# One plain gate/up step in place of two at the head of the second feed-forward half

## The chip, the cores and the metric

The kernel runs on one core of a Trainium2 chip. The metric is the device time of one launch in microseconds (us). The kernel before took 1154.8 us, the median of three runs from 1154.61 to 1155.35 us; the execution that was profiled took 1154.97 us.

Four engines do the work. PE multiplies matrices and writes to PSUM banks of 128 x 512 numbers; PEld is its weight loading. DVE does elementwise work on two operands, ACT does activations and casts, POOL little here. SP only issues transfers between device memory and on-chip memory. Each engine runs its own instructions strictly in the order in which the program lists them, and waits on semaphores for the others.

## The reference

One decoder layer with 512 tokens of width 1024, in float32:

```
x = x + 0.5 * swiglu(rms_norm(x, ffn1_norm), w_gate1, w_up1, w_down1)
h = rms_norm(x); z = h @ w_in            # gates, gMLP, q, k, v
m = sigmoid(g_a) * (y_a @ P_A) + sigmoid(g_b) * (y_b @ P_B)
x = x + m @ w_out
x = x + 0.5 * swiglu(rms_norm(x, ffn2_norm), w_gate2, w_up2, w_down2)

swiglu(h) = (silu(h @ w_gate) * (h @ w_up)) @ w_down     # hidden width 2816
```

The change is in the last line, the second feed-forward half.

## The kernel before

**Arithmetic.** A float32 product is made of three PE passes: each operand is split into a high part (`hi`, a cast on ACT, line 139) and a rest (`lo = src - hi`, a subtraction on DVE, line 140), and hi x hi, hi x lo and lo x hi are accumulated (`mm3`, lines 124 to 127; in `quad`, line 324).

**A feed-forward half** is `ffn`. The hidden width 2816 is 22 blocks of 128, taken two at a time: 11 steps, numbered q = 0 to 10. A step computes gate and up for two blocks and leaves the activated product in `a_hi[q]`, `a_lo[q]`. After the steps 0 to 3, 4 to 7 and 8 to 10 the eight down projections (line 375) follow. Loads of weights are issued by SP into `w_raw` tiles.

There are two kinds of step, and the argument `plain` says how many of the first steps are of the first kind:

- `plain_quad(q)`: for each of the two blocks, gate and up are accumulated over all 8 slices of the input with `mm3`, 512 columns a matmul: 2 x 8 x 2 x 3 = 96 matmuls of 512 columns. It needs the scaled input `xg_hi`, `xg_lo`, four loads and four splits of weights.
- `quad(q)`: a Strassen-Winograd scheme with 2 x 2 blocks (two halves of the input width, two halves of the tokens; gate and up play the other pair). It makes seven products in place of eight, each of 24 matmuls of 256 columns: 168 in all. Four of the products are with `S0` to `S3`, sums of quarters of the scaled input; four of the seven weights are sums (`total`, line 311, `w_sum` tiles, on DVE). Seven weights are split. The products come in the order A11, S1, S2, A22, S0, A12, S3. The first product goes into bank `a`, is copied out (`kept`, line 331, on ACT), and S2 is then accumulated on top of it in the same bank; S1 goes into bank `c`.

The sums S0 to S3 are made once for a half, by `add_sums` (lines 214 to 230): for each of four slices kt, one ACT scaling (line 222), four DVE operations of 256 columns (lines 224 to 227) into a tile `sums`, and then a split of 1024 columns into `s_hi` (ACT) and `s_lo` (DVE). The calls stand behind the last plain step (lines 372 to 374); one split holds all four sums of its slice, so the product S1 needs `s_hi` and `s_lo` of all four slices.

**What stands around the change.** The mixing stage ends with eight output projections (`add_out`), which leave the new input in tiles `x1` and its scaled parts in `xg_hi`, `xg_lo`. `plain_quad(0)` starts at once. Before its second block it runs `norm_scale` (lines 198 to 204), which makes `r_bc`, the reciprocal norm of each token: two PE matmuls, two ACT operations and three on DVE (lines 159 to 161). At its end each plain step does per block a DVE multiplication by `r_bc` (line 299), a Silu on ACT (line 300), a DVE multiplication (line 301), and then the split into `a_hi`, `a_lo`.

**What sets the order.** The code is written in program order, and a scheduler of the framework distributes it: by priorities and modelled durations it fixes at build time the order on each engine. So an operation of a later step can be placed ahead of one of an earlier step, and matmuls of two products can alternate. On the chip that order is then fixed. Weight tiles (`w_hi`, `w_lo`) are taken in turn from four places, `w_raw` from six, `w_sum` from two.

Of the kernel before, what the change touches and what calls it, by code (L numbers as in the profile page):

```python
# [58 lines left out]
def decoder_block(  # L59
# [434 lines left out]
    x1 = []  # L494
# [462 lines left out]
    with tc.tile_pool(name="ff2", bufs=1) as ff2:  # L957
        def finish2(j, y, ts):
            nc.sync.dma_start(out=out[:, j, ts], in_=y)

        def again2(t, j):
            nc.sync.dma_start(out=t, in_=x2_dram[j])

        ffn(ff2, gu2, dn2, 2, x1, finish2, None, {0: (norm_scale, lambda: None)}, again2, 2)


# [79 lines left out]
```

## Time and profile before

| | us |
|---|---|
| median of three runs | 1154.8 |
| profiled execution | 1154.97 |
| its span, first to last instruction | 1153.3 |
| PE busy | 1145.2 (99%) |
| DVE busy | 845.9 (73%) |
| ACT busy | 590.7 (51%) |
| POOL busy | 28.6 (2%) |
| outside the span | 1.7 |

The busy time of PE is modelled from pipelined matmuls that overlap each other: the time that a matmul costs is the distance from its start to the start of the next. The same holds in small for DVE and ACT, where a row begins a little before the one ahead of it ends. The granted clock is full (1.00) in all stretches up to the end of the kernel's work. In the second half, `plain_quad(0)` starts at 802.34 us, `plain_quad(1)` at 825.09 us, `quad(2)` at 847.38 us and `quad(3)` at 867.29 us.

### The profile page before, as it was taken

Reading aid. Unit: us, or ns where it says so; the run is one execution under the profiler, and the core shown is the slowest. Engines: PE = TensorE matmul, PEld = TensorE weight load, DVE = VectorE, ACT = ScalarE, POOL = GpSimd, SP = SyncE. Lnnn points to the kernel's source line nnn. Section 1 sums busy time; section 2 is a strip of 40 time slices with the busy share of each in tenths; the row PEclk is TensorE's granted clock in tenths of the full one; section 3 lists DMA queues with packets and bytes.
Section 4 is the critical chain, followed back from the end, with each engine's and each line's share of the span. In section 5 each row is a group of like instructions: output and inputs, shape, how many; then the busy total and the mean of one; then the engine's idle time right before and its main releaser. Section 6 shows DMA issues by size and latency. Waiting matters only on the chain.

```text
span 1153.3 us, 16684 instructions
## 1 busy us (share of the span) xinstructions
PE 1145.2 (99%) x6568; PEld 996.8 (86%) x6568; DVE 845.9 (73%) x1374; ACT 590.7 (51%) x856; POOL 28.6 (2%) x57
## 2 busy tenths in 40 slices
PE   8999999999999999999999999999999999999998
PEld 7898899989987888888878887888899899988997
DVE  6985489768876767867878976655887369877874
ACT  6653356414544554667587966334545235523440
POOL 0000000000002000000000000000000000000000
PEclk9999999999999999999999999999999999999999
DMA  8144132623324323222212124334424223541222
GB/s 276 53 132 143 55 116 75 227 64 110 90 94 147 118 74 92 74 92 74 74 55 73 56 79 160 92 123 163 152 74 147 73 74 110 166 148 67 87 82 73
DMA packets 46861, 122.08 MB, mean 106 GB/s; under 512 B 4560, under 2 KB 5856, under 8 KB 46784
## 3 DMA queue, kind: packets, MB, share of 16 engines
q1 hardware_dynamic: 44208, 113.26, 30.7%
q0 software_dynamic: 2432, 7.75, 2.0%
q8 instruction: 51, 0.84, 0.3%
q14 instruction: 26, 0.21, 0.1%
q10 hardware_dynamic: 144, 0.01, 0.0%
HBM read 114.72 MB, written 6.29 MB: 105 GB/s over the span
## 4 chain that ended last, share of the span: by engine, by line
PE 95%; ACT 2%; DMA 1%; DVE 1%; issue 0%; SPq 0%; ACTq 0%; DVEq 0%
PE bank_acc L324 20%; PE bank_att L324 11%; PE bank_acc L127 11%; PE bank_acc L125 11%; PE bank_acc L126 11%; PE bank_att L127 5%; PE bank_att L126 5%; PE bank_att L125 5%; PE bank_acc L537 4%; PE bank_acc L539 4%; PE bank_acc L538 4%; DMA w_raw<-in_gu 1%; PE bank_att L667 1%; PE bank_att L668 1%; PE bank_att L695 1%
## 5 line engine op out<-in xcount | busy, mean ns | idle before, releaser
L139 ACT CAST w_hi<-w_raw 128x1024 fp32r<-128x1024 f32 (+2 forms) x192 | 191.8, 1004 | 281.2 <-PE bank_acc L126 91.8
L140 DVE TENSOR_TENSOR w_lo<-w_raw,w_hi 128x1024 fp32r<-128x1024 f32 (+2 forms) x192 | 224.0, 1170 | 78.2 <-ACT w_hi L139 73.3
L139 ACT CAST w_hi<-w_sum 128x1024 fp32r<-128x1024 f32 x72 | 75.5, 1050 | 138.7 <-PE bank_acc L324 62.0
L324 PE MATMUL bank_acc<-s_lo,w_hi 128*128 128x256 f32 x432 | 121.6, 281 | 0.0
L324 PE MATMUL bank_acc<-s_hi,w_hi 128*128 128x256 f32 x432 | 121.5, 281 | 0.0
L324 PE MATMUL bank_acc<-s_hi,w_lo 128*128 128x256 f32 x432 | 121.4, 281 | 0.0
L140 DVE TENSOR_TENSOR w_lo<-w_sum,w_hi 128x1024 fp32r<-128x1024 f32 x72 | 87.6, 1220 | 26.0 <-ACT w_hi L139 26.0
L125 PE MATMUL bank_acc<-xg_hi,w_hi 128*128 128x512 f32 x224 | 89.3, 399 | 1.3 <-ACT w_hi L139 1.3
L127 PE MATMUL bank_acc<-xg_hi,w_lo 128*128 128x512 f32 x224 | 89.2, 398 | 1.0 <-DVE w_lo L140 1.0
L537 PE MATMUL bank_acc<-w_hi,xg_hi 128*128 128x512 f32 x224 | 88.9, 397 | 0.0
L126 PE MATMUL bank_acc<-xg_lo,w_hi 128*128 128x512 f32 x224 | 88.8, 396 | 0.0
L538 PE MATMUL bank_acc<-w_lo,xg_hi 128*128 128x512 f32 x224 | 88.6, 395 | 0.0
L539 PE MATMUL bank_acc<-w_hi,xg_lo 128*128 128x512 f32 x224 | 88.5, 395 | 0.0
L324 PEld LDWEIGHTS bank_acc<-s_hi,w_hi 128*128 128x128 f32 x432 | 81.6, 189 | 0.0
L324 PEld LDWEIGHTS bank_acc<-s_hi,w_lo 128*128 128x128 f32 x432 | 81.7, 189 | 0.0
L324 PEld LDWEIGHTS bank_acc<-s_lo,w_hi 128*128 128x128 f32 x432 | 81.6, 189 | 0.0
L125 PE MATMUL bank_acc<-a_hi,w_hi 128*128 128x512 f32 (+1 forms) x182 | 71.1, 391 | 0.0
L126 PE MATMUL bank_acc<-a_lo,w_hi 128*128 128x512 f32 (+1 forms) x182 | 71.1, 391 | 0.0
L127 PE MATMUL bank_acc<-a_hi,w_lo 128*128 128x512 f32 (+1 forms) x182 | 71.1, 391 | 0.0
L126 PE MATMUL bank_att<-a_lo,w_hi 128*128 128x512 f32 (+1 forms) x176 | 68.7, 391 | 0.0
L125 PE MATMUL bank_att<-a_hi,w_hi 128*128 128x512 f32 (+1 forms) x176 | 68.7, 391 | 0.0
L127 PE MATMUL bank_att<-a_hi,w_lo 128*128 128x512 f32 (+1 forms) x176 | 68.7, 390 | 0.0
(270 smaller groups left out, 2847.2 us busy)
## 6 DMA issues: line engine op xcount, KB each, us to landing
w_raw<-in_gu SPq DMA_DIRECT2D x86, 512.0 KB, 3.8
w_raw<-in_dn SPq DMA_DIRECT2D x32, 512.0 KB, 3.8
w_raw<-in_w_qk SPq DMA_DIRECT2D x16, 512.0 KB, 3.6
w_raw<-in_dn SPq DMA_DIRECT2D x16, 384.0 KB, 3.1
w_raw<-in_w_v SPq DMA_DIRECT2D x8, 512.0 KB, 3.6
w_raw<-in_w_ga SPq DMA_DIRECT2D x8, 512.0 KB, 3.5
w_raw<-in_w_gb SPq DMA_DIRECT2D x8, 512.0 KB, 3.7
w_raw<-in_w_pb SPq DMA_DIRECT2D x8, 512.0 KB, 3.5
```

The costliest lines, as they stand in the source:

```text
L125: nc.tensor.matmul(ps, lhsT=lhi, rhs=rhi, start=first, stop=False)
L126: nc.tensor.matmul(ps, lhsT=lhi, rhs=rlo, start=False, stop=False)
L127: nc.tensor.matmul(ps, lhsT=llo, rhs=rhi, start=False, stop=last)
L139: latest["hi"] = nc.scalar.copy(hi, src)
L140: latest["lo"] = nc.vector.tensor_tensor(lo, src, hi, op=ALU.subtract)
L324: nc.tensor.matmul(o, lhsT=l[:, s], rhs=r, start=first and f == kt == i == 0, stop=kt == HK - 1 and i == 2, skip_group_check=True,)
L537: nc.tensor.matmul(banks[t], lhsT=xg_hi[k][:, ts], rhs=hi[:, s], start=k == 0, stop=False)
L538: nc.tensor.matmul(banks[t], lhsT=xg_hi[k][:, ts], rhs=lo[:, s], start=False, stop=False)
L539: nc.tensor.matmul(banks[t], lhsT=xg_lo[k][:, ts], rhs=hi[:, s], start=False, stop=k == KD - 1)
L667: nc.tensor.matmul(s[m], lhsT=qd[m][:, qs], rhs=kd[m][:, :w], start=True, stop=False)
L668: nc.tensor.matmul(s[m], lhsT=ql[m][:, qs], rhs=kd[m][:, :w], start=False, stop=True)
L695: nc.tensor.transpose(ps[:, j * P : (j + 1) * P], a[:, j * P : (j + 1) * P], ident)
```

## The change

In the second feed-forward half the number of plain steps goes from two to one. Step 0 stays plain; step 1, which was plain, is made by `quad`, and `add_sums` is called behind step 0. Steps 2 to 10, the down projections and the first half, which keeps its two plain steps, are written as before.

```diff
@@ -961,7 +961,7 @@
         def again2(t, j):
             nc.sync.dma_start(out=t, in_=x2_dram[j])
 
-        ffn(ff2, gu2, dn2, 2, x1, finish2, None, {0: (norm_scale, lambda: None)}, again2, 2)
+        ffn(ff2, gu2, dn2, 2, x1, finish2, None, {0: (norm_scale, lambda: None)}, again2, 1)
```

The change moves instructions on all engines from step 1 on. Three places follow.

On PE, the first matmuls with the sums. In the kernel before they are those of product S1 in `quad(2)`, behind the 24 of A11; `w_hi_8033` is the weight of S1:

```order
L324 MATMUL bank_att_7999<-s_hi0_7952,w_hi_8033 128x256 [waits Activation_49]
L324 MATMUL bank_att_7999<-s_lo0_7953,w_hi_8033 128x256
L324 MATMUL bank_att_7999<-s_hi0_7952,w_lo_8034 128x256 [waits DVE_49]
L324 MATMUL bank_att_7999<-s_hi1_7963,w_hi_8033 128x256
L324 MATMUL bank_att_7999<-s_lo1_7964,w_hi_8033 128x256
L324 MATMUL bank_att_7999<-s_hi1_7963,w_lo_8034 128x256
```

In the changed kernel they are in `quad(1)`, again behind the 24 of A11. Slices 0 and 1 of S1, two matmuls of S2 and the one with `s_hi` of slice 2 come first; then, with `w_hi_7898` the weight of S1 and `w_hi_7930`, `w_lo_7931` that of S2:

```order
L324 MATMUL bank_att_7864<-s_lo2_7840,w_hi_7898 128x256 [waits DVE_49]
L324 MATMUL bank_att_7864<-s_hi2_7839,w_lo_7899 128x256
L324 MATMUL bank_acc_7863<-s_hi0_7817,w_lo_7931 128x256 [waits DVE_49]
L324 MATMUL bank_acc_7863<-s_hi1_7828,w_hi_7930 128x256
L324 MATMUL bank_acc_7863<-s_lo1_7829,w_hi_7930 128x256
L324 MATMUL bank_acc_7863<-s_hi1_7828,w_lo_7931 128x256
L324 MATMUL bank_acc_7863<-s_hi2_7839,w_hi_7930 128x256
L324 MATMUL bank_acc_7863<-s_lo2_7840,w_hi_7930 128x256
L324 MATMUL bank_acc_7863<-s_hi2_7839,w_lo_7931 128x256
L324 MATMUL bank_att_7864<-s_hi3_7850,w_hi_7898 128x256 [waits Activation_49]
L324 MATMUL bank_acc_7863<-s_hi3_7850,w_hi_7930 128x256
L324 MATMUL bank_att_7864<-s_lo3_7851,w_hi_7898 128x256 [waits DVE_49]
```

Matmuls of S1 and S2 alternate now, and each slice of the sums has waits of its own. Ahead of the matmul with `s_lo3_7851` stand 44 of the step's 168.

On DVE, what stands between the sums of slice 1 and the last of slice 3, before:

```order
L226 SCALAR_TENSOR_TENSOR sums_7967<-x1_6_7060,neg_gains_82,sums_7967 128x256
L224 SCALAR_TENSOR_TENSOR sums_7978<-x1_3_7054,gains_79,scratch_7979 128x256
L227 SCALAR_TENSOR_TENSOR sums_7967<-x1_6_7060,neg_gains_82,sums_7967 128x256
L225 SCALAR_TENSOR_TENSOR sums_7978<-x1_7_7062,gains_79,scratch_7979 128x256
L226 SCALAR_TENSOR_TENSOR sums_7978<-x1_7_7062,neg_gains_82,sums_7978 128x256
L311 TENSOR_TENSOR w_sum_8031<-w_raw_7990,w_raw_7991 128x1024
L140 TENSOR_TENSOR s_lo2_7975<-sums_7967,s_hi2_7974 128x1024
L299 TENSOR_TENSOR g_7810<-bank_att_7817,r_bc_116 128x512
L227 SCALAR_TENSOR_TENSOR sums_7978<-x1_7_7062,neg_gains_82,sums_7978 128x256
L140 TENSOR_TENSOR w_lo_8002<-w_raw_7989,w_hi_8001 128x1024
L301 SCALAR_TENSOR_TENSOR g_7810<-bank_acc_7818,g_7810 128x512
L140 TENSOR_TENSOR s_lo3_7986<-sums_7978,s_hi3_7985 128x1024
```

The same place on DVE in the changed kernel (`w_lo_7931` and `w_lo_7963` are weights of S2 and A22, `w_sum_7991` the weight sum for S0):

```order
L226 SCALAR_TENSOR_TENSOR sums_7832<-x1_6_7060,neg_gains_82,sums_7832 128x256
L224 SCALAR_TENSOR_TENSOR sums_7843<-x1_3_7054,gains_79,scratch_7844 128x256
L227 SCALAR_TENSOR_TENSOR sums_7832<-x1_6_7060,neg_gains_82,sums_7832 128x256
L225 SCALAR_TENSOR_TENSOR sums_7843<-x1_7_7062,gains_79,scratch_7844 128x256
L140 TENSOR_TENSOR a_lo0_7807<-g_7661,a_hi0_7806 128x1024
L140 TENSOR_TENSOR s_lo2_7840<-sums_7832,s_hi2_7839 128x1024
L226 SCALAR_TENSOR_TENSOR sums_7843<-x1_7_7062,neg_gains_82,sums_7843 128x256
L140 TENSOR_TENSOR w_lo_7931<-w_sum_7928,w_hi_7930 128x1024
L227 SCALAR_TENSOR_TENSOR sums_7843<-x1_7_7062,neg_gains_82,sums_7843 128x256
L140 TENSOR_TENSOR w_lo_7963<-w_sum_7960,w_hi_7962 128x1024
L311 TENSOR_TENSOR w_sum_7991<-w_raw_7854,w_raw_7855 128x1024
L140 TENSOR_TENSOR s_lo3_7851<-sums_7843,s_hi3_7850 128x1024
```

The two pieces begin at the same operation and end at `s_lo3`; weight work of the seven-product step stands in the second where work of the plain step stood in the first, and ahead of the piece `s_lo0` and `s_lo1` are now followed directly by line 301.

On ACT, the casts around the first copy out of a bank in the changed kernel:

```order
L300 ACTIVATE g_7661<-g_7661 128x512 [waits DVE_49]
L139 CAST w_hi_7962<-w_sum_7960 128x1024 [waits PE_49]
L331 COPY scratch_7894<-bank_acc_7863 128x512 [waits PE_49,Activation_49]
L139 CAST a_hi0_7806<-g_7661 128x1024 [waits DVE_49]
L139 CAST s_hi2_7839<-sums_7832 128x1024 [waits DVE_49]
L139 CAST s_hi3_7850<-sums_7843 128x1024 [waits DVE_49]
```

The copy of the first product (line 331) stands ahead of `a_hi0` and of `s_hi2`. In the kernel before `a_hi0` and `s_hi2` came right behind the Silu and the cast of a raw weight, and the first copy much later.

## Rows read from the trace of the kernel before

**Rows 1.** The page: busy time, granted clock, chain by engine

```profile
PE 1145.2 (99%) x6568; PEld 996.8 (86%) x6568; DVE 845.9 (73%) x1374; ACT 590.7 (51%) x856; POOL 28.6 (2%) x57
...
PEclk9999999999999999999999999999999999999999
...
PE 95%; ACT 2%; DMA 1%; DVE 1%; issue 0%; SPq 0%; ACTq 0%; DVEq 0%
```

**Rows 2.** Waits of PE, whole kernel: total us, times, longest us

```profile
PE bank_acc L125 <- ACT w_hi L139: 1.3, 1, 1.3
```

**Rows 3.** PE timeline, steps 1 to 3: start us, us, line, tiles

```profile
825.09 0.40 PE L125 MATMUL bank_att<-xg_hi,w_hi 128*128 128x512 f32 x1
...
847.38 0.28 PE L324 MATMUL bank_acc<-xg_hi,w_hi 128*128 128x256 f32 x1
...
850.22 0.28 PE L324 MATMUL bank_att<-s_hi,w_hi 128*128 128x256 f32 x1
...
867.29 0.28 PE L324 MATMUL bank_acc<-xg_hi,w_hi 128*128 128x256 f32 x1
```

**Rows 4.** DVE timeline in steps 0 and 1, [idle before <- what ended it]

```profile
813.93 2.36 DVE L140 TENSOR_TENSOR w_lo<-w_raw,w_hi 128x1024 fp32r<-128x1024 f32 x2 [3.98 <-PE bank_att L195]
817.41 0.69 DVE L159 SCALAR_TENSOR_TENSOR scratch<-r_bc 128x512 f32<-128x512 f32 x1 [1.12 <-ACT r_bc L203]
...
824.61 0.69 DVE L299 TENSOR_TENSOR g<-bank_att,r_bc 128x512 f32<-128x512 f32 x1
825.21 1.22 DVE L140 TENSOR_TENSOR s_lo<-sums,s_hi 128x1024 fp32r<-128x1024 f32 x1
...
827.48 0.68 DVE L301 SCALAR_TENSOR_TENSOR g<-bank_acc,g 128x512 f32<-128x512 f32 x1
...
830.35 1.22 DVE L140 TENSOR_TENSOR a_lo<-g,a_hi 128x1024 fp32r<-128x1024 f32 x1
831.49 0.48 DVE L226 SCALAR_TENSOR_TENSOR sums<-x,neg_gains,sums 128x256 f32<-128x256 f32 x1
831.88 0.48 DVE L224 SCALAR_TENSOR_TENSOR sums<-x,gains,scratch 128x256 f32<-128x256 f32 x1
...
839.06 1.22 DVE L140 TENSOR_TENSOR s_lo<-sums,s_hi 128x1024 fp32r<-128x1024 f32 x1 [0.25 <-ACT s_hi L139]
```

**Rows 5.** ACT timeline, casts and first copy of step 2

```profile
828.20 1.05 ACT L139 CAST a_hi<-g 128x1024 fp32r<-128x1024 f32 x1 [1.23 <-DVE g L301]
...
846.71 2.00 ACT L139 CAST w_hi<-w_sum 128x1024 fp32r<-128x1024 f32 x2 [7.68 <-PE bank_att L126]
...
850.42 0.59 ACT L331 COPY scratch<-bank_acc 128x512 f32<-128x512 f32 x1 [1.18 <-PE bank_acc L324]
850.90 1.06 ACT L139 CAST a_hi<-g 128x1024 fp32r<-128x1024 f32 x1
```

**Rows 6.** Loads of seven-product weights by SP, 780 to 900 us

```profile
DMA to landing us min/median/max: 3.3/3.7/4.5
```

**Rows 7.** PE timeline at the kernel's start

```profile
1.14 2.93 PE L156 MATMUL bank_att<-ones_r 128*128 128x128 f32 x12 [1.14 <-DVE eps_col L151]
5.40 0.79 PE L125 MATMUL bank_acc<-xg_hi,w_hi 128*128 128x512 f32 x1 [1.33 <-ACT w_hi L139]
...
7.27 0.63 PE L126 MATMUL bank_att<-xg_lo,w_hi 128*128 128x512 f32 x1
7.70 0.63 PE L127 MATMUL bank_att<-xg_hi,w_lo 128*128 128x512 f32 x1
...
8.95 0.39 PE L126 MATMUL bank_acc<-xg_lo,w_hi 128*128 128x512 f32 x1
9.18 0.39 PE L127 MATMUL bank_acc<-xg_hi,w_lo 128*128 128x512 f32 x1
```

**Rows 8.** Windows: busy us by engine, granted clock, DMA share, GB/s

```profile
5.40:8.95 3.55, 3.55 (x9) 2.88 (x9) 2.27 (x5) 2.14 (x5) 0.00 (x0) 1.00 0.91 299
847.55:867.45 19.90, 19.90 (x170) 19.90 (x170) 18.35 (x19) 10.54 (x14) 0.00 (x0) 1.00 0.34 107
```
## The prediction

> **What bounds the kernel now.** I read the page first. PE is busy for 99% of the span, the chain that ended last lies 95% on PE, and the granted clock is full in every slice [rows 1]. PE's waits say the same: the longest in the whole kernel is 1.3 us, at its start [rows 2]; in the second half there is none. So what the change does to PE's sequence counts in full, and what it does to DVE, ACT or the loads counts only where PE comes to wait for it.
>
> Next the PE timeline of the steps around the change [rows 3], read by starts. The plain step 1 runs from 825.09 to 847.38 us, 22.29 us for 96 matmuls of 512 columns. The seven-product step 2 runs from 847.38 to 867.29 us, 19.91 us for 168 matmuls of 256 columns, 0.1185 us each; its first product takes 2.84 us, to 850.22. Both are unbroken.
>
> Then DVE [rows 4], since the sums S0 to S3 come from there. It waits 3.98 us until 813.93, takes up the norm at 817.41 and from then on has no gap until 838.8: the row at 839.06 has the next, 0.25 us. In that stretch the last `s_lo` begins only at 839.06. That costs nothing in the kernel before, where PE has a second plain step to do until 847.38 and asks for the sums at 850.22, 10 us later. The change takes this cover away.
>
> **The change, part by part.**
>
> *PE work.* Step 1 costs 19.91 in place of 22.29 us: -2.38 us, if PE gets everything in time.
>
> The Trainium skill (TensorE: Matmul & The Clock Gate, section "Back-to-back issue gap") gives the isolated spacing at the high clock as columns over 2.4 GHz plus 2.5 ns, an estimate of 0.2158 and 0.1092 us. The two steps would then be 20.7 and 18.3 us and the gain 2.37 us; the rows are slower on both sides, and the difference is the same.
>
> *The sums on DVE.* Same 16 operations and four splits as before, but now wanted at once. PE begins step 1 at 825.09 with A11, which needs no sums, and is through at 825.09 + 2.84 = 827.93. The matmul that first needs `s_lo` of slice 3 is the 45th of the step (the order shows 44 ahead of it); unhindered it would start at 825.09 + 44 x 0.1185 = 830.30.
>
> When is that `s_lo` ready? I follow DVE's new order with spacings from rows: 1.14 us for 1024 columns (830.35 to 831.49), 0.60 for 512 (824.61 to 825.21), 0.39 for 256 (831.49 to 831.88) [rows 4].
>
> Up to 824.61 nothing moves: the DVE idle time before 813.93 takes up two of the new weight sums; a third falls behind the two splits at 813.93 and ends by 813.93 + 2 x 1.14 + 1.14 = 817.35, just ahead of the norm at 817.41, which hangs on ACT. The line-299 operation at 824.61 uses the last bank of step 0, which is unchanged. From 825.21: `s_lo` of slices 0 and 1 (2 x 1.14, to 827.49), line 301 (0.60, to 828.09), four of 256 columns (to 829.65).
>
> Then `a_lo0`, which needs `a_hi0` from ACT. There the copy of the first product now stands ahead of it. In step 2 that copy started 0.20 us after the next product's first matmul (850.42 against 850.22) and blocked ACT for 0.48 [rows 3, 5]: here from 828.13 to 828.61. `a_hi0` takes 1.05, to 829.66, so DVE loses almost nothing to it. `s_hi` of slice 2 follows 0.95 later (half of the 846.71 pair less its overlap, [rows 5]) and is ready at 830.6, in time for DVE.
>
> From 829.70: `a_lo0` to 830.84, `s_lo` of slice 2 to 831.98, one of 256 to 832.37, the split of the S2 weight to 833.51, one of 256 to 833.90, the split of the A22 weight to 835.04, the weight sum for S0 to 836.18; then `s_lo` of slice 3, which has its `s_hi` from ACT by 835.1 and takes the full 1.22: 837.40, and PE goes on at about 837.45.
>
> PE waits on the way for `s_hi` 2 (about 1.6 us), `s_lo` 2 (1.3), the S2 weight (1.3), `s_hi` 3 (0.6) and `s_lo` 3 (2.0), but only the last end counts: 837.45 - 830.30 = +7.15 us. That S2's matmuls were drawn into the holes of S1 is in this figure already, as they are among the 44.
>
> *Behind it.* The other 124 matmuls end at 837.45 + 124 x 0.1185 = 852.14, against 847.38 before. No further wait: the A12 weight is wanted at 852.14 - 2 x 2.84 = 846.5, and DVE reaches its split by 842.4 even though it must first wait for the next step's weights. These loads wait for a `w_raw` tile until the S0 weight sum ends at 836.2, land 3.7 us later [rows 6], and two operations of 1.14 follow. PE wants them in product S1 of step 2, after 855. Steps 2 and on are as before, shifted; the accumulators of the down projections change places between the two bank pools, which costs nothing where each has four banks.
>
> *Unknowns.* The handoffs of semaphores between DVE, ACT and PE at five new waits: 0 (the chain is DVE's, which never stops) to +0.5 us (0.1 each); I take the 0.05 in the sum. The new weight sums ahead of the norm could be late by their loads and push DVE's chain: 0 to +0.5; I take 0. Changed bank pools: -0.1 to +0.3; I take 0.
>
> *Sum.* -2.38 + 7.15 = +4.77. Against the profiled execution, 1154.97, that is 1159.7; its median stands 0.17 lower, so the forecast is 1159.6 us.
>
> **Rivals.**
>
> *A: the clock falls in the holes.* From 828.8 to 837.4 PE has 14 matmuls, 1.7 us of work in 8.6. What the clock does then, the trace before shows only at the kernel's start: after an idle stretch of 1.33 us that ended at 5.40, 512 columns took 0.43 us (7.27 to 7.70), and from 8.95 on 0.23 [rows 7]: the lower of the two levels, 1.2 GHz, for 3.55 us, although the granted clock of that window reads 1.00 [rows 8]. If PE comes out of the holes at that level for as long again, it does half of 3.55 us: +1.8 us, 1161.4; twice as long would be 1163.2. For it: the holes. Against it: at the start PE came from nothing, here from 800 us of dense work, and the longest single hole is 2.0 us.
>
> [...] No run here yet shows a gap of this size in mid-kernel.
>
> *B: the sums are there in time.* Then only the PE term is left: 1154.8 - 2.4 = 1152.4, faster. Its mechanism: ACT and DVE use the time in which `x1` is complete and DVE is idle, before 813.93 [rows 4]. It decides from `s_lo` of slice 3 ending at 830.2; the two terms cancel when it ends at 832.7. For that, the four weight and `a_lo0` operations ahead of it (4 x 1.14 = 4.6 us) would have to stand behind it. The fixed order says they don't, and the sums stand behind the norm as before.
>
> *C: the delay spreads.* DVE is busy for 18.35 of the 19.90 us of a seven-product step [rows 8], so it wins back only 1.5 us a step on PE. If it came out of the holes late itself, `quad(2)` would wait again: up to one DVE operation per product, 1 to 2 us, 1161. Against it: PE is held up by DVE, so DVE is level with it, and each product then leaves 2.84 us for one split and part of a sum.
>
> **How the numbers follow.** Forecast 1159.6: 0.58; by its unknowns it alone lies between 1158.8 and 1160.8. A: 0.25. C: 0.07. A stall of half the size, from an order or handoff that I misread (1156): 0.05. B: 0.05. The range that leaves out 2 in 10 is 1158.3 to 1162.0: it holds the forecast, C and the nearer part of A. A measurement of this kernel can tell 0.2%, 2.3 us, from no change: faster is B (0.05), the same is half of the halved stall (0.03), slower all else (0.92).
>
> **What would show it.** PE in the profile after: step 1 from 825.09, A11 without a break, then waits on `s_hi` and `s_lo` of slices 2 and 3 and on the S2 weight, some 7 us in total over five or six waits, the last ending at 837.4; step 2 beginning at 852.1 and every later step at the same distance from its neighbours as before. For A: 256-column matmuls spaced 0.24 us instead of 0.12 after 837.4. I am wrong if step 2 starts before 849.7, or if PE shows waits after 838.

## The result, and the profile after

The changed kernel takes 1161.44 us (median of four runs, 1160.96 to 1162.7), the kernel before on the same chip 1154.7 us (four runs). The ratio is 1.0057, with a 95% interval from 1.0045 to 1.0070: slower by 6.7 us. The forecast was 1159.6 us with a range from 1158.3 to 1162.0. The time lies inside, 1.8 us above the forecast and at the value of rival A.

The profiled execution took 1161.1 us. Its page shows PE busy 1.8 us more than in [rows 1], a dip of one tenth in the granted clock in the 29th of the 40 slices, and 3% of the chain on ACT where it had 2%:

```profile
PE 1147.0 (99%) x6640; PEld 1001.9 (86%) x6640; DVE 856.0 (74%) x1383; ACT 595.2 (51%) x861; POOL 28.6 (2%) x57
...
PEclk9999999999999999999999999999899999999999
...
PE 94%; ACT 3%; DVE 2%; issue 1%; DMA 0%; DVEq 0%; ACTq 0%
```

PE's waits over the whole kernel (line waited for: total us, times, longest). The first line answers to [rows 2]; the other three are new, and all four of their waits lie in step 1:

```profile
PE bank_acc L125 <- ACT w_hi L139: 1.5, 1, 1.5
...
PE bank_att L324 <- DVE s_lo L140: 2.6, 2, 1.5
...
PE bank_att L324 <- ACT s_hi L139: 1.4, 1, 1.4
...
PE bank_acc L324 <- DVE w_lo L140: 1.0, 1, 1.0
```

They add up to 5.0 us, less than the 6.7 us that were lost, although the step itself became 2.4 us shorter in work. The rest has to be read from distances between starts. The PE timeline of step 1 (start, us; in brackets the idle time ahead and what ended it):

```profile
824.76 0.28 PE L324 MATMUL bank_acc<-xg_hi,w_hi 128*128 128x256 f32 x1
...
827.60 0.28 PE L324 MATMUL bank_att<-s_hi,w_hi 128*128 128x256 f32 x1
...
828.71 0.28 PE L324 MATMUL bank_acc<-s_lo,w_hi 128*128 128x256 f32 x1
830.38 0.39 PE L324 MATMUL bank_att<-s_hi,w_hi 128*128 128x256 f32 x1 [1.39 <-ACT s_hi L139]
831.83 0.38 PE L324 MATMUL bank_att<-s_lo,w_hi 128*128 128x256 f32 x1 [1.06 <-DVE s_lo L140]
832.05 0.28 PE L324 MATMUL bank_att<-s_hi,w_lo 128*128 128x256 f32 x1
833.36 0.58 PE L324 MATMUL bank_acc<-s_hi,w_lo 128*128 128x256 f32 x1 [1.03 <-DVE w_lo L140]
833.74 0.41 PE L324 MATMUL bank_acc<-s_hi,w_hi 128*128 128x256 f32 x1
833.95 0.41 PE L324 MATMUL bank_acc<-s_lo,w_hi 128*128 128x256 f32 x1
...
837.16 0.58 PE L324 MATMUL bank_att<-s_lo,w_hi 128*128 128x256 f32 x1 [1.51 <-DVE s_lo L140]
837.54 0.41 PE L324 MATMUL bank_att<-s_hi,w_lo 128*128 128x256 f32 x1
837.75 0.41 PE L324 MATMUL bank_att<-s_hi,w_hi 128*128 128x256 f32 x1
...
840.10 0.33 PE L324 MATMUL bank_att<-s_hi,w_lo 128*128 128x256 f32 x1
840.27 0.28 PE L324 MATMUL bank_acc<-s_lo,w_hi 128*128 128x256 f32 x1
840.38 0.28 PE L324 MATMUL bank_acc<-s_hi,w_lo 128*128 128x256 f32 x1
...
841.93 0.39 PE L324 MATMUL bank_att<-xg_hi,w_hi 128*128 128x256 f32 x1
842.15 0.28 PE L324 MATMUL bank_att<-xg_lo,w_hi 128*128 128x256 f32 x1
...
853.40 0.28 PE L324 MATMUL bank_acc<-xg_hi,w_hi 128*128 128x256 f32 x1
```

Three things are to be seen. A11 is unbroken (824.76 to 827.60, 2.84 us, as in [rows 3]). Then there are four holes, and PE goes on for good at 837.16, when slice 3 of `s_lo` is there: this is the 45th matmul, and it starts 12.40 us behind the first. And from 833.36 to 840.27 the matmuls stand 0.21 us apart (833.74, 833.95) in place of 0.12 (840.27, 840.38). The windows of the same stretch show why (busy us by engine, then the granted clock):

```profile
828.00:832.00 4.00, 1.52 (x8) 0.92 (x8) 4.00 (x7) 2.33 (x3) 0.00 (x0) 1.00 0.00 0
832.00:836.00 4.00, 2.62 (x11) 2.12 (x11) 4.00 (x6) 1.05 (x1) 0.00 (x0) 0.67 0.00 0
836.00:840.00 4.00, 2.84 (x13) 2.84 (x14) 2.60 (x3) 1.04 (x1) 0.00 (x0) 0.50 0.71 241
840.00:844.00 4.00, 4.00 (x34) 3.95 (x34) 3.02 (x3) 3.08 (x4) 0.00 (x0) 0.98 0.21 33
```

The granted clock fell to 0.50, the level of 1.2 GHz, after the three holes between 829 and 833.4 us, and was back at the full 2.4 GHz soon after 840. The "busy" 2.84 us of the third window are 13 slow matmuls.

DVE in the same stretch. It is without a gap until the weight split behind the last `s_lo` ends (4.00 us busy of 4.00 in the first two windows), and its order is the one read before the run:

```profile
824.88 2.35 DVE L140 TENSOR_TENSOR s_lo<-sums,s_hi 128x1024 fp32r<-128x1024 f32 x2
827.15 0.68 DVE L301 SCALAR_TENSOR_TENSOR g<-bank_acc,g 128x512 f32<-128x512 f32 x1
...
829.41 1.22 DVE L140 TENSOR_TENSOR a_lo<-g,a_hi 128x1024 fp32r<-128x1024 f32 x1
830.56 1.22 DVE L140 TENSOR_TENSOR s_lo<-sums,s_hi 128x1024 fp32r<-128x1024 f32 x1
...
832.09 1.22 DVE L140 TENSOR_TENSOR w_lo<-w_sum,w_hi 128x1024 fp32r<-128x1024 f32 x1
...
833.62 1.22 DVE L140 TENSOR_TENSOR w_lo<-w_sum,w_hi 128x1024 fp32r<-128x1024 f32 x1
834.75 1.22 DVE L311 TENSOR_TENSOR w_sum<-w_raw 128x1024 f32<-128x1024 f32 x1
835.89 1.22 DVE L140 TENSOR_TENSOR s_lo<-sums,s_hi 128x1024 fp32r<-128x1024 f32 x1
...
839.70 1.23 DVE L311 TENSOR_TENSOR w_sum<-w_raw 128x1024 f32<-128x1024 f32 x1 [1.40 <-DMA w_raw<-in_gu]
```

From the first `s_lo` (824.88) to the start of the last (835.89) are 11.01 us; in the working of the prediction they were 10.97 (825.21 to 836.18).

**The account.** All times are now taken from the first matmul of `plain_quad(0)`, so that what differs at the kernel's start drops out. The first down projection comes 84.87 us later in the kernel before and 91.24 in the changed one (+6.37), the last matmul 346.85 and 353.19 us later (+6.34): all of it is lost in step 1, and nothing of it is lost or won back later. Its parts:

- the work of the step: 19.91 in place of 22.29 us, -2.38;
- the stall until `s_lo` of slice 3: 12.40 less 44 x 0.1185 = 5.21, +7.19;
- 14 matmuls at the lower clock, 837.16 to 840.27 (0.38 us from the first to the second, 0.21 between the others): 3.11 in place of 14 x 0.1185 = 1.66 us, +1.45;
- the first matmul of A22 at 841.93, whose bank was copied out by ACT until 841.87 (0.58 from 841.29): its successor comes 0.22 later in place of 0.12, +0.10.

The sum is +6.36 us. ACT's row for the last part:

```profile
841.29 0.58 ACT L331 COPY scratch<-bank_att 128x512 f32<-128x512 f32 x1
```

### The profile page after: what moved, and what is told of

Read it like the earlier page. It is cut to its first block, busy times and chain, and to the rows that moved or that the text cites. A ratio compares the mean times of both kernels' runs of the same rounds, so it can differ in the third digit from the quotient of the medians.

```text
span 1159.3 us, 16850 instructions
## 1 busy us (share of the span) xinstructions
PE 1147.0 (99%) x6640; PEld 1001.9 (86%) x6640; DVE 856.0 (74%) x1383; ACT 595.2 (51%) x861; POOL 28.6 (2%) x57
## 4 chain that ended last, share of the span: by engine, by line
PE 94%; ACT 3%; DVE 2%; issue 1%; DMA 0%; DVEq 0%; ACTq 0%
PE bank_acc L324 21%; PE bank_att L324 12%; PE bank_acc L125 10%; PE bank_acc L127 10%; PE bank_acc L126 10%; PE bank_att L126 5%; PE bank_att L127 5%; PE bank_att L125 5%; PE bank_acc L539 4%; PE bank_acc L537 4%; PE bank_acc L538 4%; PE bank_att L667 1%; PE bank_att L668 1%; PE bank_att L695 1%; ACT q L641 0%
## 5 line engine op out<-in xcount | busy, mean ns | idle before, releaser
L324 PE MATMUL bank_acc<-s_hi,w_lo 128*128 128x256 f32 x456 | 128.7, 282 | 1.0 <-DVE w_lo L140 1.0
L324 PE MATMUL bank_acc<-s_hi,w_hi 128*128 128x256 f32 x456 | 128.8, 282 | 0.0
L324 PE MATMUL bank_acc<-s_lo,w_hi 128*128 128x256 f32 x456 | 128.6, 282 | 0.0
L140 DVE TENSOR_TENSOR w_lo<-w_sum,w_hi 128x1024 fp32r<-128x1024 f32 x76 | 92.5, 1220 | 26.1 <-ACT w_hi L139 26.1
L324 PEld LDWEIGHTS bank_acc<-s_hi,w_lo 128*128 128x128 f32 x456 | 86.6, 190 | 1.2 <-DVE w_lo L140 1.2
L324 PEld LDWEIGHTS bank_acc<-s_hi,w_hi 128*128 128x128 f32 x456 | 86.6, 190 | 0.3 <-ACT scratch L331 0.2
L324 PEld LDWEIGHTS bank_acc<-s_lo,w_hi 128*128 128x128 f32 x456 | 86.5, 190 | 0.0
L125 PE MATMUL bank_acc<-xg_hi,w_hi 128*128 128x512 f32 x208 | 83.1, 400 | 1.5 <-ACT w_hi L139 1.5
L127 PE MATMUL bank_acc<-xg_hi,w_lo 128*128 128x512 f32 x208 | 83.0, 399 | 0.0
L126 PE MATMUL bank_acc<-xg_lo,w_hi 128*128 128x512 f32 x208 | 82.7, 397 | 0.0
```

The source lines that it names most:

```text
L125: nc.tensor.matmul(ps, lhsT=lhi, rhs=rhi, start=first, stop=False)
L126: nc.tensor.matmul(ps, lhsT=lhi, rhs=rlo, start=False, stop=False)
L127: nc.tensor.matmul(ps, lhsT=llo, rhs=rhi, start=False, stop=last)
L140: latest["lo"] = nc.vector.tensor_tensor(lo, src, hi, op=ALU.subtract)
L324: nc.tensor.matmul(o, lhsT=l[:, s], rhs=r, start=first and f == kt == i == 0, stop=kt == HK - 1 and i == 2, skip_group_check=True,)
```

## The experiments

The theory was the forecast's, with rival A on top: the sums stand too late on DVE, the stall is set by the end of `s_lo` of slice 3, and the lower clock behind it is a second term. Where the expectations number the theories, this is Theory 1. Against it stand that the seven-product step costs more in itself when it comes so early (Theory 2), and that the clock has no part in the loss (Theory 3). Two runs move the sums, one keeps PE fed, one makes DVE's chain longer. The kernel before took 1154.64 us beside them (21 runs).

### The sums made earlier, one plain step

The calls of `add_sums` in the second half are moved from behind `plain_quad(0)` to its middle, ahead of the norm. The input `x1` is complete there.

```diff
                     if q == 0 and f == 1 and k == 0:
+                        if load is None:
+                            for kt in range(HK):
+                                add_sums(kt, xt[kt], xt[kt + HK])
                         prepare[0][0](); prepare[0][1]()
...
-                if q == plain - 1:
+                if q == plain - 1 and load is not None:
                     for kt in range(HK):
                         add_sums(kt, xt[kt], xt[kt + HK])
```

> One plain step as in the changed kernel, but the sums are written ahead of the norm inside plain step 0, so that DVE makes them while PE still has the second block of step 0 to do. Theory 1 (PE lost its time in the holes behind the late sums, and those holes cost it the clock as well): no holes, step 1 unbroken, clock full, only the 2.4 us of saved matmuls left: 1152.3 us, 0.2% faster than the kernel before. Theory 2 (what the seven-product step itself costs DVE, ACT and the loads spreads into later steps): still slower than before, 1156 to 1159 us.

Measured: 1152.0 us (11 runs), ratio to the kernel before 0.9978 [0.9969, 0.9987]. It is faster than both kernels. In its DVE timeline the last slice of `s_lo` ends at 821.46 us, ahead of step 1, and the norm's last operation comes behind it and still in time:

```profile
820.25 1.21 DVE L140 TENSOR_TENSOR s_lo<-sums,s_hi 128x1024 fp32r<-128x1024 f32 x1
821.38 0.68 DVE L160 TENSOR_TENSOR scratch<-scratch 128x512 f32<-128x512 f32 x1
...
823.12 0.68 DVE L161 SCALAR_TENSOR_TENSOR r_bc<-scratch,r_bc 128x512 f32<-128x512 f32 x1
...
824.86 1.28 DVE L302 TENSOR_TENSOR g<-bank_att,r_bc 128x512 f32<-128x512 f32 x2
```

On its PE step 1 is unbroken, 19.91 us from its first matmul to that of step 2:

```profile
824.43 0.28 PE L327 MATMUL bank_acc<-xg_hi,w_hi 128*128 128x256 f32 x1
...
827.27 0.28 PE L327 MATMUL bank_att<-s_hi,w_hi 128*128 128x256 f32 x1
...
844.34 0.28 PE L327 MATMUL bank_acc<-xg_hi,w_hi 128*128 128x256 f32 x1
```

Counted from the first matmul of `plain_quad(0)`, the last one comes 2.31 us earlier than in the kernel before. So the -2.38 us of the work were there to be had, the step in itself costs nothing more, and the whole loss of the change came from where the sums stand.

### The sums made earlier, two plain steps

The same edit to the kernel before.

> The kernel before, two plain steps, with the sums written early as in the other run. Theory 1: PE has no wait either way, so no change, 1154.7 us within 0.5. A rival, that early sums cost or win something by themselves (the norm comes some 3 us later on DVE): over 1 us from 1154.7.

Measured: 1154.69 us (11 runs), ratio 1.0001 [0.9992, 1.0009]; the last matmul stands 346.86 us behind the first of step 0, against 346.85. Moving the sums alone is worth nothing: with two plain steps they are 10 us early anyway. The gain above is that of the saved work, which the earlier sums let through.

### PE kept busy through the holes

48 matmuls of 256 columns into a free bank, whose result nobody reads, are put behind A11 in step 1 of the changed kernel. DVE and ACT are left alone.

```diff
             product(a, b11, "A11", True)
             p1 = kept(a)
+            if q == 1 and load is None:
+                for _ in range(FILL):
+                    nc.tensor.matmul(e[:, :HT], lhsT=ones_r, rhs=xg_hi[0][:, :HT], start=True, stop=True)
             t3 = total(b12, b22)
```

> The changed kernel with 48 idle matmuls of 256 columns, on operands that are long ready, between product A11 and product S1 of step 1; their result is overwritten unread. DVE and ACT keep their order. They fill 5.7 us of the holes. Theory 1: the late s_lo of slice 3 still sets when PE goes on, but PE comes out at the full clock, so the 14 matmuls behind it are spaced 0.12 us and not 0.21: 1.4 to 1.7 us faster than the changed kernel, about 1159.8 us. Theory 3 (the clock has no part, the excess over the forecast is handoffs and later waits): as slow as the changed kernel, 1161.4, or slower.

Measured: 1159.77 us (five runs), ratio 1.0045 [1.0032, 1.0058]. With more work on PE it is 1.7 us faster than the changed kernel by the medians; its slowest run (1160.92) lies just below the fastest of the changed kernel (1160.96). The granted clock over the whole run is 0.999 or 1.000 in all five runs, against 0.995 or 0.996 in all four of the changed kernel. Its PE timeline around the idle matmuls (line 342) and the one wait of over 0.1 us that is left in this step:

```profile
823.65 0.28 PE L325 MATMUL bank_acc<-xg_hi,w_hi 128*128 128x256 f32 x1
...
826.48 5.76 PE L342 MATMUL bank_att<-xg_hi,ones_r 128*128 128x256 f32 x48
832.08 0.28 PE L325 MATMUL bank_att<-s_hi,w_hi 128*128 128x256 f32 x1
...
836.07 0.39 PE L325 MATMUL bank_att<-s_lo,w_hi 128*128 128x256 f32 x1 [1.11 <-DVE s_lo L141]
836.29 0.28 PE L325 MATMUL bank_att<-s_hi,w_lo 128*128 128x256 f32 x1
836.41 0.28 PE L325 MATMUL bank_att<-s_hi,w_hi 128*128 128x256 f32 x1
```

and the windows with the granted clock:

```profile
832.00:836.00 4.00, 2.87 (x23) 2.46 (x21) 4.00 (x6) 2.10 (x2) 0.00 (x0) 1.00 0.01 3
836.00:840.00 4.00, 3.94 (x32) 3.88 (x33) 2.51 (x4) 1.92 (x3) 0.00 (x0) 1.00 0.77 260
```

PE goes on 12.42 us behind the first matmul of the step, as in the changed kernel (12.40): that point is DVE's, whatever PE does before it. But the clock is 1.00 and the spacing 0.12 us at once. The last matmul stands 351.87 us behind the first of step 0, 1.32 us earlier than in the changed kernel. The lower clock had cost 1.45; 0.10 goes to a second matmul that starts late after a wait (836.07 to 836.29, 0.22), beside the first one of A22 (839.49 to 839.72).

### DVE's chain made longer

The subtraction that makes `s_lo` of slice 3 is done a second time, with the same result.

```diff
             split(s_hi[kt], s_lo[kt], f)
+            if norm == 2 and kt == HK - 1:
+                nc.vector.tensor_tensor(s_lo[kt], f, s_hi[kt], op=ALU.subtract)
```

> The changed kernel with the DVE subtraction that makes s_lo of slice 3 done twice; with the weight split that stands between, the last one ends 2.3 us later. Theory 1 (DVE's chain alone sets when PE goes on): the last hole is 2.3 us longer and the time 2.3 us, if the clock comes back at the same distance from the end of the holes: 1163.7 us. Rival (the end of the holes is set by ACT, or by PE's own restarts): under 0.5 us, 1161.4 to 1161.9.

Measured: 1163.43 us (four runs), ratio 1.0077 [1.0063, 1.0090]. On DVE the second subtraction (line 232) stands one weight split behind the first, so the chain is two operations longer:

```profile
835.49 1.22 DVE L140 TENSOR_TENSOR s_lo<-sums,s_hi 128x1024 fp32r<-128x1024 f32 x1
836.68 1.22 DVE L140 TENSOR_TENSOR w_lo<-w_sum,w_hi 128x1024 fp32r<-128x1024 f32 x1
837.83 1.22 DVE L232 TENSOR_TENSOR s_lo<-sums,s_hi 128x1024 fp32r<-128x1024 f32 x1
```

PE follows it to 839.10, 14.74 us behind the first matmul of its step 1 (824.36):

```profile
839.10 0.58 PE L326 MATMUL bank_att<-s_lo,w_hi 128*128 128x256 f32 x1 [3.85 <-DVE s_lo L232]
...
843.05 0.28 PE L326 MATMUL bank_acc<-s_hi,w_lo 128*128 128x256 f32 x1
```

The stall is 14.74 - 5.21 = 9.53 us, 2.34 more than in the changed kernel. The lower clock lasts longer too: 18 matmuls from 839.10 to 843.05 took 3.95 us in place of 2.13, +1.82. With the work's -2.38 that is +8.97; the last matmul stands 355.80 us behind the first of step 0, +8.95.

### The runs side by side

Us, against the kernel before. The terms and the last matmul are from the traces, the last column from the medians (the changed kernel's from its own comparison).

| kernel | work | stall | lower clock | late first matmuls | sum | last matmul | median |
|---|---|---|---|---|---|---|---|
| changed | -2.38 | 7.19 | 1.45 | 0.10 | 6.36 | 6.34 | 6.7 |
| changed, PE kept busy | -2.38 | 7.21 | 0 | 0.20 | 5.03 | 5.02 | 5.1 |
| changed, longer chain | -2.38 | 9.53 | 1.82 | 0 | 8.97 | 8.95 | 8.8 |
| changed, early sums | -2.38 | 0 | 0 | 0 | -2.38 | -2.31 | -2.6 |
| before, early sums | 0 | 0 | 0 | 0 | 0 | 0.01 | 0.05 |

## Why the prediction was right, and where it was not

**PE work, -2.38 us.** Right: step 1 with its sums in time takes 19.91 us, and the run with early sums ends 2.31 us earlier in the trace. Step 0 takes 0.09 us longer there (22.84 in place of 22.75), which covers the difference of 0.07.

**The sums on DVE, +7.15 us.** Right in place and size, 7.19. The step's first matmul came at 824.76 in place of 825.09, since the kernel ran 0.33 us ahead from its start, and everything moved with it. The chain of 15 operations from `s_lo` of slice 0 to that of slice 3, worked out from the order and three spacings, was 0.04 us too short. The two runs show that this chain, and nothing on PE, sets the point at which PE goes on: a longer chain moves it by 2.34 us, more work on PE by 0.02.

**The waits on the way.** For `s_hi` 2, `s_lo` 2, the S2 weight, `s_hi` 3 and `s_lo` 3 the prediction had 1.6, 1.3, 1.3, 0.6 and 2.0 us; the trace has 1.39, 1.06, 1.03, none and 1.51. A row counts the idle time from the modelled end of the matmul ahead; by starts, less 0.12, the waits are 1.55, 1.33, 1.19, none and 1.81. The last two shrank because the matmuls ahead of them ran at half the clock and so filled part of the wait. That cost nothing: the last end decides, as the prediction says. The new waits come to 5.0 us in the list and to 5.88 by starts; the rest of the 7.19 for which PE was held up is the slow matmuls ahead of 837.16 (0.93) and single matmuls that started late around the holes (0.38).

**"No further wait" behind it.** Nearly right. The A22 product waited for ACT's copy of S1's bank, which the prediction did not look at: `s_lo` of slice 3 lets S1 and S2 end close together. It costs 0.10 us. From 853.40 on the steps run as before (39.85 us to the first down projection, 39.83 before), so rival C did not occur.

**The clock.** This is the step that failed. The forecast took the full clock behind the holes and gave rival A 0.25; A is what happened, beside a stall that was sized right. Of the 1.57 us that the forecast's +4.77 lacks against the last matmul's +6.34, the clock makes 1.45. By its own unknowns the forecast reached only 1160.8; that 1161.44 lies in the range is due to the nearer part of A, for which the range was drawn wider.

A's working has three parts. That PE comes out of the holes at the lower level: right. That it stays there for as long as at the kernel's start, 3.55 us: nearly, it was 3.11 us from 837.16 on, and 3.95 in the run with the longer chain. That 256 columns are then spaced 0.24, and half of the time is lost: 0.213; with the shorter time 1.45 us were lost and not 1.8. With its own +6.57 us A came within 0.2 us of the last matmul's +6.34. That its 1161.4 meets the median is in part luck: its clock term was 0.35 too large, and the median moved by 0.4 more than the last matmul. The argument against A was that PE came from 800 us of dense work and that no single hole was over 2.0 us. The changed kernel shows that neither protects it, and the run with PE kept busy that the holes are the cause: the same delay with one hole of 1.11 us left the clock at 1.00, while three holes of 1.39, 1.06 and 1.03 us with only a few matmuls between them brought it to 0.50. Whether the length of the holes or the little work between them decides was not separated.

For the lower clock the Trainium skill (TensorE: Matmul & The Clock Gate, "Back-to-back issue gap") gives a spacing of the columns over 1.2 GHz, an estimate of 0.2133 us for 256. The trace agrees with it by the 0.213. The prediction had doubled the row of the full clock, 0.1185 us, and so came to 0.24.

**Rival B.** Wrong for this order, as forecast: `s_lo` of slice 3 ended at 837.11 (835.89 + 1.22), far behind the point at which the terms cancel. But its mechanism is real: with the calls written earlier the time is 1152.0, where B had 1152.4. DVE's time ahead of 813.93 [rows 4] holds most of the sums, not all: in that run 12 of their 16 operations and two of the four `s_lo` start before it, and the last `s_lo` ends at 821.46.

## What to carry to other kernels

A step removed from a sequence that keeps one engine busy can also remove the cover of what was made beside it: before it goes, look up when the next step's operands are ready, and move their making ahead first. An operand's end is found by adding the fixed order of its engine with the spacings of a trace, here to 0.04 us in 11. Where PE then has several holes close together, weigh a term for the clock: here it was paid on the matmuls behind the last hole (1.45 us), and PE work that nobody needs was cheaper than the holes.

## What had not been expected of the hardware

- The clock fell to 0.50 in the middle of the kernel though the holes ahead of it were only 1.39, 1.06 and 1.03 us long (the one behind it 1.51). The last matmul ahead of the third hole is still a fast one (0.28 us at 832.05), the first behind it a slow one (0.58 us at 833.36), and the full clock came back 3.1 us after PE had gone on for good (3.9 in the run with the longer chain).
- At the lower clock 256 columns are 0.213 us apart, 1.80 times the 0.1185 at the full clock, not twice.
- The successor of a matmul that starts after a wait comes 0.10 us late at the full clock (0.22 behind it in place of 0.12 at 831.83 and 841.93; 0.22 and 0.23 in the run with PE kept busy).
